# Convolution taps and norm gain loaded as rows and transposed, decay rows laid out by head, and the decay add ordered behind the convolution of k

## The chip, the cores and the metric

The kernel runs on one core of a Trainium2 chip. The metric is device time in microseconds (us) of one execution; lower is better. Three runs of the kernel before gave 1844.48, 1847.61 and 1849.42 us (median 1847.61).

## What is computed

One encoder block on a float32 sequence of 1024 tokens by 1024 channels. Two token mixers read the same normalised input: a gated linear attention (GLA) and a gated DeltaNet (GDN). Their sum is projected and added to the input; a mixture of experts with 32 experts follows, then a last RMSNorm. The change touches the norm's gain and the GDN branch, whose part of the reference is, shortened:

```python
h = rms_norm(x, norm1_w)
proj = h @ w_in
# GDN: centred depthwise convolution of 5 taps on q, k and v, then silu
qkv = silu(centred_depthwise_conv(concat([dq, dk, dv]), conv_w))   # conv_w: [5, 3072]
q, k = l2_norm(q) * dk ** -0.5, l2_norm(k)                         # 8 heads of 128
g = -exp(a_log) * softplus(a + dt_bias)                            # per head and direction
# per chunk, with g the cumulative sum inside the chunk
decay = exp(where(tri, g[..., :, None] - g[..., None, :], 0.0))
lower = strict_lower(k_beta @ k.T * decay)
attn = tri(q @ k.T * decay)
# forward and backward directions, summed
```

## The kernel before, in words

The work is written as straight Python on tiles, and a planner orders it when the program is built: for each engine it makes one fixed list of instructions, by program order and by its own estimate of when operands are ready. On the chip each engine takes its list in order, so an instruction whose operand is late holds everything behind it on that engine. All plain loads and stores are issued by SyncE (SP), also in a fixed order.

Stages: (1) lines 133 to 167 load x in 8 tiles, normalise the rows, turn them with TensorE and split the result into a high and a low part `hT_hi`, `hT_lo`; the norm's gain `n1` is applied per partition at L165 and L166. (2) Lines 205 to 253 make the gates of all GDN heads at once: `gcs` holds the cumulative gates with tokens on partitions and columns in the order direction, chunk, head. TensorE turns it (L249), VectorE copies it out (L251) and SP stores it to device memory as `gcs_d` (L252), one row of 128 floats for each (direction, chunk, head). (3) For each of 8 heads `gdn_stage1` (L282) projects k, convolves it, normalises it, then q, then v, and solves the triangular systems on VectorE; `gdn_stage2` (L400) runs the recurrence over 8 chunks in both directions, and `gdn_stage3` (L498) normalises and stores. Stage 3 of the head before is called inside stage 1 through `finish` (L333). Between the heads `gate_task` (L258) adds projections that only TensorE is long busy with: one behind head 0's stage 1, one behind its stage 2, and two behind each later head while they last. (4) GLA, the output projection, routing, the experts, the last norm.

Each projection (`proj`, L118) is 48 matmuls of 128x128 on 128x512 into two accumulators `pj` (two buffers). Its weights come as two units of 256 KB through `load_w` (L103): load `wraw` (three buffers), cast on ScalarE to `whi` (L112), subtract on VectorE to `wlo` (L114); a later `wraw` load waits for an earlier subtraction.

The convolution (`conv`, L283): ScalarE copies the two accumulators into `cin` (one buffer, L289); VectorE makes one multiply (L292) and four multiply-adds (L294) over 128x1024, each with a tap from `cw[:, wi, j]` as a per-partition scalar; ScalarE takes tanh (L300) and VectorE finishes the silu (L301). TensorE then turns the result for the norm (`sumsq`, L311). `cw` is filled by five loads of one tap each (L188) and `n1` by one (L134); in all six the channel goes to the partition, so consecutive elements in device memory land on different partitions.

The decay (L340 to L346): for each head, half of the chunks (`hf`) and direction (`d`), SP loads four rows of `gcs_d` into `e`, each repeated over all 128 partitions (L342; 128 partitions times 4 runs of 512 bytes, 256 KB); VectorE adds the mask `mneg` (L344); ScalarE takes four exponentials (L346). `e` then scales the Gram matrix of k into `m` (L348), and later the scores of q (L364). `e` has seven buffers, so the loads of the next head's first three tiles are issued as soon as buffers come free.

The lines that set where the add stands:

```python
ka = conv("k", C_DK)
rk, pts = sumsq("k", ka)
...
if finish:
    finish()
...
e = gd.tile([P, 4, P], F32, name="e", bufs=7)
nc.sync.dma_start(e, dap(gcs_d, ...))
ve.tensor_tensor(e, e, mneg[d]..., op=OP.add)
```

Of the kernel before, what the change touches and what calls it, by code (L numbers as in the profile page):

```python
# [8 lines left out]
F32 = mybir.dt.float32  # L9
# [4 lines left out]
OP = mybir.AluOpType  # L14
# [4 lines left out]
P = 128  # L19
D = 1024  # L20
T = 1024
NT = T // P
KD = D // P
# [11 lines left out]
def hybrid_kernel(ctx: ExitStack, tc: tile.TileContext, ins, out):  # L35
# [6 lines left out]
    def dap(t, off, dims):  # L42
        return bass.AP(tensor=t.tensor, offset=t.offset + off, ap=dims)
# [51 lines left out]
    with mix:  # L95
# [34 lines left out]
            return res  # L130


        n1 = cst.tile([P, KD], F32, name="n1")
        nc.sync.dma_start(n1, ins["norm1_w"][0].rearrange("(k p) -> p k", p=P))  # L134
        with tc.tile_pool(name="xp", bufs=1) as xp:
            xt = []
            ssx = xp.tile([P, NT], F32, name="ssx")
            junk = xp.tile([P, D], F32, name="junk", bufs=2)
            for t in range(NT):
                xx = xp.tile([P, D], F32, name=f"xx{t}")  # L140
                nc.sync.dma_start(xx, x[t * P:(t + 1) * P, :])
                xt.append(xx)

            def scale(q):

                for t in (2 * q, 2 * q + 1):
                    sc.activation(junk, xt[t], AF.Square, accum_out=ssx[:, t:t + 1])
                v = small.tile([P, 2], F32, name="vx")
                ve.tensor_scalar(v, ssx[:, 2 * q:2 * q + 2], 1.0 / D, EPS, op0=OP.mult, op1=OP.add)
                rx = rsqrt(v, 2, "x")  # L150
                for i in range(2):
                    t = 2 * q + i
                    ve.tensor_scalar(xt[t], xt[t], rx[:, i:i + 1], None, op0=OP.mult)

            for q in range(4):
                scale(q)
            wfirst = load_w(None, [(0, C_GL, 96), (96, C_AB, 32)])
            for q in range(2):
                for k in range(KD):
                    pt = bank(("tp", "mg")[k % 2], 2)  # L160
                    for i in range(4):
                        te.transpose(pt[:, i, :], xt[4 * q + i][:, k * P:(k + 1) * P], ident)
                    s = slice(q * 512, q * 512 + 512)
                    pf = pt.rearrange("p a b -> p (a b)")
                    sc.activation(hT_hi[:, k, s], pf, AF.Copy, scale=n1[:, k:k + 1])  # L165
                    ve.scalar_tensor_tensor(hT_lo[:, k, s], pf, n1[:, k:k + 1],  # L166
                                            hT_hi[:, k, s].bitcast(F32), op0=OP.mult, op1=OP.subtract)
# [15 lines left out]
        gdn_nw = cst.tile([P, 1], F32, name="gdn_nw")  # L183
        nc.sync.dma_start(gdn_nw, ins["gdn_norm_w"].rearrange("o c -> c o"))
        ve.tensor_scalar(gdn_nw, gdn_nw, 0.25, None, op0=OP.mult)
        cw = cst.tile([P, 24, 5], F32, name="cw")
        for j in range(5):
            nc.sync.dma_start(cw[:, :, j], ins["gdn_conv_w"][0, j].rearrange("(k p) -> p k", p=P))  # L188


        NBs = cst.tile([P, 2, NT, GDN_H], F32, name="NBs")
# [5 lines left out]
        with tc.tile_pool(name="gate", bufs=1) as gpool:  # L197
            glrT = gpool.tile([P, T], F32, name="glrT")
            abT = gpool.tile([P, T], F32, name="abT")
            dt_b = gpool.tile([P, 2, GDN_H], F32, name="dt_b")  # L200
            na = gpool.tile([P, 2, GDN_H], F32, name="na")
            for i, s in enumerate(("fwd", "bwd")):
                nc.sync.dma_start(dt_b[:, i], pbcast(ins[f"gdn_dt_bias_{s}"], GDN_H))
                nc.sync.dma_start(na[:, i], pbcast(ins[f"gdn_a_log_{s}"], GDN_H))
            ps = proj(None, wfirst)
            for hf in range(2):
                s = slice(hf * 512, hf * 512 + 512)
                sc.copy(glrT[0:32, s], ps[hf][0:32])
                ve.tensor_copy(abT[96:128, s], ps[hf][96:128])
            nc.sync.dma_start(glr_d, glrT[0:32])  # L210

            pab = psum.tile([P, NT, 32], F32, name="pab", tag="mg", bufs=2)
            for t in range(NT):
                te.transpose(pab[:, t], abT[96:128, t * P:(t + 1) * P], ident[96:128, 96:128])
            z = gpool.tile([P, 2, 2, NT, GDN_H], F32, name="zg")
            u = gpool.tile([P, 2, 2, NT, GDN_H], F32, name="ug")
            ve.tensor_tensor(z[:, 0].rearrange("p i c h -> p c i h"),
                             pab[:, :, 0:16].rearrange("p c (i h) -> p c i h", i=2),
                             dt_b[:, None, :, :].to_broadcast([P, NT, 2, GDN_H]), op=OP.add)
            ve.tensor_scalar(z[:, 1].rearrange("p i c h -> p c i h"),  # L220
                             pab[:, :, 16:32].rearrange("p c (i h) -> p c i h", i=2), -1.0, None,
                             op0=OP.mult)

            sc.activation(u, z, AF.Abs)
            sc.activation(u, u, AF.Exp, scale=-1.0)
            sc.activation(u, u, AF.Ln, bias=1.0)
            ve.scalar_tensor_tensor(u, z, 0.0, u, op0=OP.max, op1=OP.add)
            sc.activation(na, na, AF.Exp)
            g = gpool.tile([P, 2, NT, GDN_H], F32, name="gg")
            for i in range(2):  # L230
                ve.scalar_tensor_tensor(g[:, i], u[:, 0, i], -1.0,
                                        na[:, i, None, :].to_broadcast([P, NT, GDN_H]),
                                        op0=OP.mult, op1=OP.mult)
            pg = psum.tile([P, 2, 2, NT * GDN_H], F32, name="pg", tag="mg", bufs=2)
            for i in range(2):
                gi = g[:, i].rearrange("p c h -> p (c h)")
                te.matmul(pg[:, 0, i], tri[i], gi, start=True, stop=True)
                te.matmul(pg[:, 1, i], ones, gi, start=True, stop=True)
            fl = lambda t: t.rearrange("p i c h -> p i (c h)")
            ve.tensor_copy(fl(gcs), pg[:, 0])  # L240
            sc.activation(fl(DEC), pg[:, 1], AF.Exp)

            ve.scalar_tensor_tensor(NBs, u[:, 1], -1.0, gcs, op0=OP.mult, op1=OP.subtract)
            ve.tensor_tensor(fl(KT), fl(NBs), pg[:, 1], op=OP.add)
            sc.activation(KT, KT, AF.Exp)
            sc.activation(EG, gcs, AF.Exp)

            prow = bank("mg", 2)
            te.transpose(prow[:, 0], gcs.rearrange("p i c h -> p (i c h)"), ident)  # L249
            grow = gpool.tile([P, P], F32, name="grow")  # L250
            ve.tensor_copy(grow, prow[:, 0])  # L251
            nc.sync.dma_start(gcs_d, grow)  # L252
            ve.tensor_scalar(NEG, EG, -1.0, None, op0=OP.mult)
# [28 lines left out]
        def gdn_stage1(h, finish=None):  # L282
            def conv(nm, c0):  # L283
                ps = proj(c0 + h * P)
                cin = gd.tile([P, T + 4], F32, name="cin", bufs=1)
                gp.memset(cin[:, 0:2], 0.0)
                gp.memset(cin[:, T + 2:T + 4], 0.0)
                for hf in range(2):
                    sc.copy(cin[:, 2 + hf * 512:2 + hf * 512 + 512], ps[hf])  # L289
                wi = {"q": 0, "k": 8, "v": 16}[nm] + h  # L290
                a = gd.tile([P, T], F32, name="acc", bufs=3)
                ve.tensor_scalar(a, cin[:, 0:T], cw[:, wi, 0:1], None, op0=OP.mult)  # L292
                for tp in range(1, 5):
                    ve.scalar_tensor_tensor(a, cin[:, tp:tp + T], cw[:, wi, tp:tp + 1], a,  # L294
                                            op0=OP.mult, op1=OP.add)

                for hf in range(2):
                    s = slice(hf * 512, hf * 512 + 512)
                    th = gt.tile([P, 512], F32, name="gth", bufs=2)
                    sc.activation(th, a[:, s], AF.Tanh, scale=0.5)  # L300
                    ve.scalar_tensor_tensor(a[:, s], th, 1.0, a[:, s], op0=OP.add, op1=OP.mult)  # L301
                return a

            def sumsq(nm, a):
# [12 lines left out]
                return rsqrt(ss, NT, nm), pts  # L317

            ka = conv("k", C_DK)
            rk, pts = sumsq("k", ka)  # L320
            ktok = gd.tile([P, NT, P], F32, name="ktok", bufs=2)
            kch = gd.tile([P, NT, P], F32, name="kch", bufs=2)
# [13 lines left out]
            for hf in range(2):  # L336
# [2 lines left out]
                    te.matmul(pgm[:, i], kch[:, 4 * hf + i], kch[:, 4 * hf + i], start=True, stop=True)  # L339
                for d in range(2):  # L340
                    e = gd.tile([P, 4, P], F32, name="e", bufs=7)
                    nc.sync.dma_start(e, dap(gcs_d, ((d * NT + 4 * hf) * GDN_H + h) * P,  # L342
                                             [[0, P], [GDN_H * P, 4], [1, P]]))
                    ve.tensor_tensor(e, e, mneg[d][:, None, :].to_broadcast([P, 4, P]), op=OP.add)  # L344
                    for i in range(4):
                        sc.activation(e[:, i], e[:, i], AF.Exp, bias=NBs[:, d, 4 * hf + i, h:h + 1])  # L346
                    m = gd.tile([P, 4, P], F32, name="m", bufs=6)
# [867 lines left out]
```

## Time and profile before

| | |
|---|---|
| median of the three runs | 1847.61 us |
| the profiled execution's own time | 1845.9 us |
| its span from first to last instruction | 1844.1 us |
| TensorE matmul busy | 1684.2 us (91% of the span) |
| VectorE busy | 1326.0 us (72%) |
| ScalarE busy | 918.2 us (50%) |
| mean granted TensorE clock | 0.974 of full speed |

The span is 1.8 us shorter than the execution's own time. Engines in the rows are PE (TensorE matmul), PEld (TensorE weight load), DVE (VectorE), ACT (ScalarE), POOL (GpSimd) and SPq (SyncE's list of loads and stores). In a timeline row the columns are the start and the duration in us, the engine, the line, the operation, output and inputs, and how many were merged; in brackets stands how long the engine was idle just before, and what ended that. Where `x` and `ns` stand, they are a count and a mean. Matmuls overlap, so the durations of single ones add up to more than the time in which they ran.

### The profile page before, as it was taken

To read this page: it belongs to the slowest core of one execution; us is meant where nothing else is said; L and a number is where in the kernel's file an instruction comes from. 1 tells how busy PE (TensorE), PEld (TensorE's weight loads), DVE (VectorE), ACT (ScalarE), POOL (GpSimd) and SP (SyncE) were. 2 spreads that over 40 slices of the span, in tenths; PEclk is the share of its full clock that TensorE was granted. 3 is DMA by queue.
4 is the path that set the end of the run, shared out by engine and by line. 5 is a ranking of instruction groups with operands and counts; after the bars stand their busy time and mean duration, and the time that the engine had idled before them with its cause. 6 is when DMAs were issued, how large, how long until landed. Compare 5 with 4: busy or idle time off the path is not lost. (4 is left out here: it accounts for less than half of the span.)

```text
span 1844.1 us, 27107 instructions
## 1 busy us (share of the span) xinstructions
PE 1684.2 (91%) x9582; PEld 1378.5 (75%) x9582; DVE 1326.0 (72%) x2998; ACT 918.2 (50%) x1913; POOL 177.6 (10%) x184
## 2 busy tenths in 40 slices
PE   6799899899999999999999999998999799888880
PEld 4587777787888888888888778887778587666660
DVE  6589695787687787877855355655778797777773
ACT  5434435254362453534434344534435687777762
POOL 0000000000000000000000000000000143334430
PEclk9899999999999999999999999999999899999996
DMA  6322223322323222231222112312677699999965
GB/s 148 64 71 61 65 55 79 69 57 77 74 58 97 52 75 69 69 93 45 66 69 74 43 44 75 95 55 78 208 230 252 215 345 312 311 321 326 330 202 199
DMA packets 236298, 241.02 MB, mean 131 GB/s; under 512 B 89136, under 2 KB 187712, under 8 KB 236160
## 3 DMA queue, kind: packets, MB, share of 16 engines
q1 hardware_dynamic: 226944, 222.46, 39.0%
q0 software_dynamic: 9216, 16.81, 4.0%
q8 instruction: 76, 1.25, 0.3%
q14 instruction: 62, 0.51, 0.1%
HBM read 205.44 MB, written 50.53 MB: 139 GB/s over the span
## 5 line engine op out<-in xcount | busy, mean ns | idle before, releaser
L80 PE MATMUL pj<-hT_hi,whi 128*128 128x512 f32 x1168 | 472.2, 404 | 2.8 <-ACT cin L289 2.4
L81 PE MATMUL pj<-hT_lo,whi 128*128 128x512 f32 x1168 | 472.3, 404 | 0.0
L82 PE MATMUL pj<-hT_hi,wlo 128*128 128x512 f32 x1168 | 471.6, 404 | 0.5 <-DVE wlo L114 0.5
L1044 DVE TENSOR_TENSOR elo<-eraw,ehi 128x2048 fp32r<-128x2048 f32 x96 | 219.5, 2288 | 70.9 <-ACT ehi L1043 68.2
L80 PEld LDWEIGHTS pj<-hT_hi,whi 128*128 128x128 f32 x1168 | 222.1, 190 | 43.9 <-ACT cin L289 3.2
L82 PEld LDWEIGHTS pj<-hT_hi,wlo 128*128 128x128 f32 x1168 | 222.0, 190 | 39.4 <-DVE wlo L114 1.2
L81 PEld LDWEIGHTS pj<-hT_lo,whi 128*128 128x128 f32 x1168 | 222.3, 190 | 37.5
L1043 ACT CAST ehi<-eraw 128x2048 fp32r<-128x2048 f32 x96 | 184.5, 1922 | 69.9 <-DMA eraw<-in_moe_w_up_dram 65.1
L112 ACT CAST whi<-wraw 128x512 fp32r<-128x512 f32 x146 | 90.6, 620 | 190.3 <-PE pj L81 177.0
L114 DVE TENSOR_TENSOR wlo<-wraw,whi 128x512 fp32r<-128x512 f32 x146 | 100.0, 686 | 93.0 <-ACT whi L112 83.8
L294 DVE SCALAR_TENSOR_TENSOR acc<-cin,cw,acc 128x1024 f32<-128x1024 f32 x96 | 122.5, 1276 | 0.7
L80 PE MATMUL pgu<-ehi,xh 128*128 128x512 f32 x256 | 105.3, 411 | 0.0
L1095 POOL DMA_INDIRECT acc_d<-y,idx x32 | 84.1, 2627 | 199.2 <-DMA acc_d<-y,idx 72.3
L81 PE MATMUL pgu<-elo,xh 128*128 128x512 f32 x256 | 102.1, 399 | 0.0
L82 PE MATMUL pgu<-ehi,xl 128*128 128x512 f32 x256 | 101.9, 398 | 0.0
L391 DVE TENSOR_TENSOR prod<-V,X 128x2 f32<-128x2 f32 (+30 forms) x248 | 85.5, 345 | 5.9
L393 DVE TENSOR_REDUCE V<-prod 128x1 f32<-128x2 f32 (+30 forms) x248 | 84.4, 340 | 6.1
L266 ACT ACTIVATE gth<-pj 128x512 f32<-128x512 f32 x64 | 38.1, 595 | 75.9 <-PE pj L82 75.4
L1050 POOL DMA_INDIRECT xb<-h_d,idx x32 | 59.2, 1850 | 149.6 <-ACT xb L1105 132.6
L346 ACT ACTIVATE e<-e,NBs 128x128 f32<-128x128 f32 x128 | 44.0, 396 | 34.0 <-DVE e L344 34.0
L473 ACT ACTIVATE kt<-ktok,KT 128x128 f32<-128x128 f32 x112 | 44.7, 402 | 30.8 <-PE cb L474 13.5
L82 PEld LDWEIGHTS pgu<-ehi,xl 128*128 128x128 f32 x256 | 48.7, 190 | 11.8
(405 smaller groups left out, 3268.2 us busy)
## 6 DMA issues: line engine op xcount, KB each, us to landing
wraw<-in_w_in_dram SPq DMA_DIRECT2D x144, 256.0 KB, 3.0
eraw<-in_moe_w_gate_dram SPq DMA_DIRECT2D x64, 512.0 KB, 15.9
eraw<-in_moe_w_up_dram SPq DMA_DIRECT2D x64, 512.0 KB, 17.7
eraw<-in_moe_w_down_dram SPq DMA_DIRECT2D x32, 1024.0 KB, 19.1
e<-gcs_d SPq DMA_DIRECT2D x32, 256.0 KB, 6.0
gate_d<-gateT SPq DMA_DIRECT2D x16, 512.0 KB, 3.6
xx<-in_x_dram SPq DMA_DIRECT2D x8, 512.0 KB, 7.7
gin<-gate_d SPq DMA_DIRECT2D x8, 512.0 KB, 3.2
```

Of the source, the lines that this page charges most:

```text
L80: te.matmul(o, lh, rh, start=start, stop=False)
L81: te.matmul(o, lh, rl, start=False, stop=False)
L82: te.matmul(o, ll, rh, start=False, stop=stop)
L112: sc.copy(hi, raw)
L114: ve.tensor_tensor(lo, raw, hi.bitcast(F32), op=OP.subtract)
L294: ve.scalar_tensor_tensor(a, cin[:, tp:tp + T], cw[:, wi, tp:tp + 1], a, op0=OP.mult, op1=OP.add)
L391: ve.tensor_tensor(pr_[:, :mc, :i + 1], V[:, :mc, :i + 1], X[:, i, :i + 1][:, None, :].to_broadcast([P, mc, i + 1]), op=OP.mult)
L393: ve.tensor_reduce(V[:, :mc, i], pr_[:, :mc, :i + 1], axis=AX.X, op=OP.add)
L1043: sc.copy(hi, raw)
L1044: ve.tensor_tensor(lo, raw, hi.bitcast(F32), op=OP.subtract)
L1050: gp.indirect_dma_start(out=xb, out_offset=None, in_=h2_d[:, :], in_offset=bass.IndirectOffsetOnAxis(ap=si, axis=0), bounds_check=T - 1, o ...
L1095: gp.indirect_dma_start(out=acc_d[:, :], out_offset=bass.IndirectOffsetOnAxis(ap=si, axis=0), in_=y, in_offset=None, bounds_check=T - 1, o ...
```

## The change

- `n1` and the taps `cw` become columns of one tile `cols` (128x128). Two loads bring 8 rows of the norm's gain and 120 rows of the taps (5 taps times 24 blocks of 128 channels), 512 bytes a row, into `rows`; TensorE turns the tile and ScalarE copies it out. These instructions stand ahead of the loads of x. The six loads of before are gone.
- Ahead of the turn of the cumulative gates VectorE copies them into the order head, direction, chunk. A row of `gcs_d` is now (head, direction, chunk), so the four rows of one `e` lie next to each other, and a load of `e` is 128 runs of 2 KB.
- The add on `e` gets an ordering edge: on VectorE it stands behind the last instruction of this head's convolution of k.

```diff
-        n1 = cst.tile([P, KD], F32, name="n1")
-        nc.sync.dma_start(n1, ins["norm1_w"][0].rearrange("(k p) -> p k", p=P))
+        cols = cst.tile([P, P], F32, name="cols")
+        n1 = cols[:, 0:KD]
         with tc.tile_pool(name="xp", bufs=1) as xp:
+            rows = xp.tile([P, P], F32, name="rows")
+            nc.sync.dma_start(rows[0:KD], ins["norm1_w"][0].rearrange("(k p) -> k p", p=P))
+            nc.sync.dma_start(rows[KD:P], ins["gdn_conv_w"][0].rearrange("j (k p) -> (j k) p", p=P))
+            pt = bank("tp", 2)
+            te.transpose(pt[:, 0], rows, ident)
+            sc.copy(cols, pt[:, 0])
...
-        cw = cst.tile([P, 24, 5], F32, name="cw")
-        for j in range(5):
-            nc.sync.dma_start(cw[:, :, j], ins["gdn_conv_w"][0, j].rearrange("(k p) -> p k", p=P))
+        def cw(i, j):
+            return cols[:, KD + 24 * j + i:KD + 24 * j + i + 1]
...
-            te.transpose(prow[:, 0], gcs.rearrange("p i c h -> p (i c h)"), ident)
+            ghead = gpool.tile([P, GDN_H, 2, NT], F32, name="ghead")
+            ve.tensor_copy(ghead.rearrange("p h i c -> p i c h"), gcs)
+            te.transpose(prow[:, 0], ghead.rearrange("p h i c -> p (h i c)"), ident)
...
-                ve.tensor_scalar(a, cin[:, 0:T], cw[:, wi, 0:1], None, op0=OP.mult)
+                ve.tensor_scalar(a, cin[:, 0:T], cw(wi, 0), None, op0=OP.mult)
...
-                    ve.scalar_tensor_tensor(a[:, s], th, 1.0, a[:, s], op0=OP.add, op1=OP.mult)
+                    conv.last = ve.scalar_tensor_tensor(a[:, s], th, 1.0, a[:, s], op0=OP.add, op1=OP.mult)
...
             ka = conv("k", C_DK)
+            k_done = conv.last.ins
...
-                    nc.sync.dma_start(e, dap(gcs_d, ((d * NT + 4 * hf) * GDN_H + h) * P,
-                                             [[0, P], [GDN_H * P, 4], [1, P]]))
-                    ve.tensor_tensor(e, e, mneg[d][:, None, :].to_broadcast([P, 4, P]), op=OP.add)
+                    nc.sync.dma_start(e.rearrange("p a b -> p (a b)"),
+                                      dap(gcs_d, ((2 * h + d) * NT + 4 * hf) * P, [[0, P], [1, 4 * P]]))
+                    with tc.issue_after(k_done):
+                        ve.tensor_tensor(e, e, mneg[d][:, None, :].to_broadcast([P, 4, P]), op=OP.add)
```

## Rows read from the trace of the kernel before

**Rows 1.** Stretches: start:end, length; busy us: PE, PEld, DVE, ACT, POOL; PEclk, DMA, GB/s.

```profile
300.00:400.00 100.00, 92.19 (x581) 76.06 (x581) 77.17 (x193) 40.62 (x118) 2.66 (x11) 0.98 0.32 73
...
700.00:800.00 100.00, 99.80 (x655) 83.33 (x654) 76.83 (x201) 47.93 (x144) 3.36 (x13) 1.00 0.28 72
```

**Rows 2.** Timeline, PE: the instructions that followed its gaps up to 451 us.

```profile
31.39 0.44 PE L162 MATMUL mg<-ident,xx 128*128 128x128 f32 x2 [2.35 <-DVE hT_lo L166]
...
78.51 0.87 PE L311 MATMUL tp<-ident,acc 128*128 128x128 f32 x3 [11.31 <-issue]
...
228.42 0.90 PE L513 MATMUL mg<-ident,oac 128*128 128x128 f32 x3 [4.08 <-DVE oac L511]
...
343.37 0.94 PE L513 MATMUL mg<-ident,oac 128*128 128x128 f32 x4 [5.12 <-DVE oac L511]
...
450.54 0.66 PE L513 MATMUL mg<-ident,oac 128*128 128x128 f32 x4 [2.02 <-DVE oac L511]
```

**Rows 3.** Timeline, ACT and DVE, 56 to 79 us: head 0's convolution of k.

```profile
56.65 0.58 ACT L289 COPY cin<-pj 128x512 f32<-128x512 f32 x1
...
58.66 0.69 DVE L344 TENSOR_TENSOR e<-e,mneg 128x512 f32<-128x512 f32 x1 [3.91 <-DMA e<-gcs_d]
...
62.40 0.69 DVE L344 TENSOR_TENSOR e<-e,mneg 128x512 f32<-128x512 f32 x1 [3.04 <-DMA e<-gcs_d]
63.01 0.74 DVE L292 TENSOR_SCALAR acc<-cin,cw 128x1024 f32<-128x1024 f32 x1
...
67.55 0.69 DVE L344 TENSOR_TENSOR e<-e,mneg 128x512 f32<-128x512 f32 x1 [0.36 <-DMA e<-gcs_d]
...
77.72 1.28 DVE L301 SCALAR_TENSOR_TENSOR acc<-gth,acc 128x512 f32<-128x512 f32 x2
```

**Rows 4.** Groups by line: busy us, mean ns, then idle before and its releaser.

```profile
L294 DVE SCALAR_TENSOR_TENSOR acc<-cin,cw,acc 128x1024 f32<-128x1024 f32 x96 | 122.5, 1276 | 0.7
...
L344 DVE TENSOR_TENSOR e<-e,mneg 128x512 f32<-128x512 f32 x32 | 22.0, 689 | 31.3 <-DMA e<-gcs_d 31.3
```

**Rows 5.** Timeline, DVE: the adds on e ahead of the gap at 224 us.

```profile
220.42 0.69 DVE L344 TENSOR_TENSOR e<-e,mneg 128x512 f32<-128x512 f32 x1 [2.11 <-DMA e<-gcs_d]
...
223.43 0.69 DVE L344 TENSOR_TENSOR e<-e,mneg 128x512 f32<-128x512 f32 x1 [1.96 <-DMA e<-gcs_d]
```

**Rows 6.** Stretches after three of the gaps (columns as in rows 1).

```profile
78.50:84.20 5.70, 5.69 (x18) 4.74 (x19) 5.56 (x7) 4.57 (x24) 0.00 (x0) 0.51 0.18 46
228.40:234.40 6.00, 5.98 (x18) 5.07 (x19) 4.91 (x12) 0.59 (x1) 0.00 (x0) 0.51 0.40 134
343.40:347.00 3.60, 3.60 (x13) 3.18 (x14) 2.54 (x6) 0.09 (x1) 0.00 (x0) 0.53 0.08 28
```

**Rows 7.** Timeline, 14 to 30 us, and the packets of 12 to 32 us.

```profile
DMA packets 19445, 1.94 MB, mean 97 GB/s; under 512 B 17771, under 2 KB 19307, under 8 KB 19444
...
23.99 3.57 SPq L109 DMA_DIRECT2D wraw<-in_w_in_dram  x3
...
29.35 0.62 ACT L112 CAST whi<-wraw 128x512 fp32r<-128x512 f32 x1 [3.55 <-DMA wraw<-in_w_in_dram]
```

**Rows 8.** DMA issues: count, KB each, median us to landing.

```profile
wraw<-in_w_in_dram SPq DMA_DIRECT2D x144, 256.0 KB, 3.0
...
e<-gcs_d SPq DMA_DIRECT2D x32, 256.0 KB, 6.0
...
n2r<-in_norm_w_dram SPq DMA_DIRECT2D x1, 512.0 KB, 5.7
```

**Rows 9.** A stretch of head 1's convolutions, and the PE gap in it.

```profile
125.00:150.00 25.00, 22.93 (x106) 18.69 (x105) 24.38 (x44) 7.34 (x20) 0.13 (x2) 1.00 0.25 68
...
146.42 0.50 PE L80 MATMUL pj<-hT_hi,whi 128*128 128x512 f32 x1 [2.06 <-ACT cin L289]
```

**Rows 10.** Timeline: a 128x128 copy on DVE, and ACT's first square.

```profile
49.76 0.29 DVE L240 COPY gcs<-pg 128x128 f32<-128x128 f32 x1 [1.06 <-PE pg L238]
...
5.06 1.06 ACT L147 ACTIVATE junk<-xx 128x1024 f32<-128x1024 f32 x1 [3.04 <-DMA xx<-in_x_dram]
```

More of the change, by code (lines that the diff above doesn't have):

```diff
@@ L291, in conv @@
                 a = gd.tile([P, T], F32, name="acc", bufs=3)
-                ve.tensor_scalar(a, cin[:, 0:T], cw[:, wi, 0:1], None, op0=OP.mult)
+                ve.tensor_scalar(a, cin[:, 0:T], cw(wi, 0), None, op0=OP.mult)
                 for tp in range(1, 5):
-                    ve.scalar_tensor_tensor(a, cin[:, tp:tp + T], cw[:, wi, tp:tp + 1], a,
+                    ve.scalar_tensor_tensor(a, cin[:, tp:tp + T], cw(wi, tp), a,
                                             op0=OP.mult, op1=OP.add)
```

## The prediction

> **What bounds the kernel now.** I first cut the span into stretches. TensorE is the bound from 500 to 1000 us: in 700 to 800 us it is busy for 99.8 of 100 us, and nothing the change does there can shorten it. Between 300 and 400 us it is busy for only 92.19 [rows 1]. So whatever there is to win lies before 500 us, and I next read TensorE's timeline there for gaps. Four of its large gaps, and one at the start, end on something that the change touches: 2.35 us at 29 us, 11.31 at 67 us, 4.08 at 224, 5.12 at 338 and 2.02 at 448 us [rows 2].
>
> The largest is named "issue", so I followed its operand `acc`, head 0's convolved k. Its inputs were complete at 57.23 us (56.65 plus 0.58). But in VectorE's list the adds on `e` stand ahead of and between the steps of the convolution, and they waited for their loads: 3.91 and 3.04 us before the first step started at 63.01, and more between the later ones; the last step came at 77.72 [rows 3]. Over the whole kernel the 32 adds cost 22.0 us of work and 31.3 us of VectorE standing still for these loads [rows 4]. The gaps at 224, 338 and 448 us wait for VectorE's L511 (stage 3 of the head before). Ahead of the first of them two adds waited 2.11 and 1.96 us, together 4.07 against a gap of 4.08 [rows 5, 2]; the same pattern of late adds stands before the other two.
>
> The gaps also cost clock. After three of them TensorE's granted clock is 0.51 to 0.53 of full speed, the lower level of 1.2 GHz, for 5.7, 6.0 and 3.6 us of nearly full work [rows 6], where a stretch without such a gap has 1.00, the level of 2.4 GHz [rows 1].
>
> The gap at 29 us has another source. From 12 to 32 us the queue moves 19,445 packets, 17,771 of them under 512 bytes [rows 7]; by the code 5 x 3072 are single taps of 4 bytes. The next weights were issued only at 23.99 us, and ScalarE stood 3.55 us until they landed at 29.35, with the split of `hT_hi` behind them in its list [rows 7].
>
> **The change part by part.**
>
> Taps and gain as rows. It removes the six loads of 4-byte elements (16,384 of them) and adds two loads of 128 rows, one turn on TensorE and one 128x128 copy on ScalarE. SP is moved past nothing but x: x is issued behind two loads instead of one, yet no longer behind 1024 single elements, and I cost that at nothing between those two. The copy is about as long as VectorE's of this size, 0.29 us, and fits in the 3.04 us that ScalarE idles before its first square [rows 10]; if the rows landed later than x, every square would start late by that. With the taps gone the weights can go as soon as a buffer is free, and ScalarE's wait should go. TensorE then gains its 2.35 us; between 0 and ScalarE's 3.55. I take -2.4.
>
> Head 0. Without adds ahead of it, the convolution takes one step of 0.74 and four of 1.276 [rows 3, 4], 5.84 us, to 63.1; two tanh and the two halves of the last step (1.28) end near 65.5. TensorE has work until about 67.2 (78.51 less 11.31), so the whole gap is covered. What is late next is the next projection's accumulator, which waits for `cin`; where that happens now in head 1, TensorE stood 2.06 us [rows 9]. So -11.3 + 2.1 = -9.2 (0 to -11.3). The 5.7 us at half clock become 2.85: -2.8 (0 to -2.85).
>
> Heads 1 to 3. The adds that waited belonged to a later head and did not have to be done yet; behind that head's convolution of k they are long landed. The gaps of 4.08, 5.12 and 2.02 us go: -11.2 (0 to -11.2). Half clock after them, (6.0 + 3.6) / 2 = -4.8 (0 to -4.8). From head 4 on TensorE is full, so nothing is won.
>
> What the moved adds cost. Three adds per head leave the recurrence, where VectorE has room, for the convolutions, where in head 1 it is busy 24.38 of 25 us [rows 9]. That is 3 x 0.689 = 2.07 us a head [rows 4]. In heads 4 to 7 TensorE's full list covers it. In heads 1 to 3 it could stand in full (6.2), or not at all; I take half, +3.1. If the cover is gone everywhere it is 7 x 2.07 = 14.5. The four exponentials of each tile follow the adds; the Gram matrix that they are needed with comes only after sum of squares, inverse root and two turns, so I cost them at nothing.
>
> Gates by head. One more strided copy on VectorE, 0.29 us by the nearest copy [rows 10], delays the store of `gcs_d` and the first `cin` copy behind it: +0.3 (0 to 1). The loads of `e` become 128 runs of 2 KB for 512 of 512 bytes. Today they take 6.0 us to landing, where weights of the same 256 KB in 512-byte runs take 3.0, so neither bytes nor packet size alone explains it; the one broadcast with long runs, 512 KB, took 5.7 [rows 8]. Between 3 and 6 us I take 3, which costs nothing more, as the adds are no longer early.
>
> By a rule of the Trainium skill ("DMA: Bandwidth & Descriptors", Anatomy of one DMA and Specifications) a load costs about 2.0 us plus its bytes over 436 GB/s, and runs of 512 bytes are already at line rate; by it longer runs would change nothing. The 6.0 against 3.0 us speak against the first half of it for this load; no row here shows the second.
>
> Sum: -2.4 - 9.2 - 2.8 - 11.2 - 4.8 + 3.1 + 0.3 = -27.0. From the profiled execution's 1845.9 that gives 1818.9; the median of the runs shown stands 1.7 above it, so I expect 1820.6, say **1820.5**. With the best ends (-3.55 - 11.3 - 2.85 - 11.2 - 4.8) it is -33.7, 1814. The planner remakes every list, and waits of one or two us come and go with that; the forecast's own range is 1808 to 1831.
>
> **The rivals.**
>
> Longer runs do not help: the loads of `e` still take 6.0 us. Then the fourth of head 0's adds, which could start at 67.55 [rows 3], is some 2.4 us behind k's end, and q's convolution behind it. For it: the same row is still read 128 times. Against: the adds are no longer in front of anything that TensorE waits for at once. 1820.5 + 2.4 = 1823. Chance 0.13. By the page's rule above the loads would not change either.
>
> The gaps of heads 1 to 3 come back as waits for `cin` in the convolutions, since VectorE is full there: 11.2 + 4.8 are lost again. For it: 24.38 of 25 us and the 2.06 us wait [rows 9]. Against: in heads 4 to 7 the same work leaves TensorE at 99.8 [rows 1]. 1836.5. Chance 0.13.
>
> The change does not do what it says: the planner puts other late work where the adds stood, or head 0 waits for the next weights instead, and only the start is won: 1847.6 - 2.4 = 1845. Against: nothing else in those lists waits for so long. Chance 0.07.
>
> Slower: in each of the eight heads four adds now stand right behind k's convolution, ahead of the inverse root that k's normalisation needs, and TensorE runs dry for 4 x 0.689 = 2.8 us and then loses 2.8 more at half clock, as after the gap of head 0 [rows 6]. 8 x 5.6 = 44.8 against 30.4 of gains (all of the terms with a minus): +14.4 and the 0.3, 1862. It decides once a head loses over 30.4 / 8 = 3.8 us. Against: the squares on ScalarE come first, and VectorE fills their time with the adds. Chance 0.09.
>
> **How the numbers follow.** Forecast 0.58, the rivals 0.13, 0.13, 0.07 and 0.09. A measurement of this kernel can tell about 0.3%, 5.5 us, from no change. Faster by more than that (under 1842): the forecast and the first two rivals, less a tail, 0.83. Within it: the third and that tail, 0.08. Slower: 0.09. The range from 1808 to 1845 leaves out the slower case, half of the third and the ends of the forecast, just under 0.2.
>
> **What would show it.** In the profile after: no load of taps between 14 and 24 us, no wait of ScalarE on `wraw` at 29; all steps of head 0's convolution together on VectorE, the turn of k at 63 to 65 us without a gap before it; the adds' wait for `e` down from 31.3 us to under 5; no gap of over 2 us before L513; TensorE's clock at full speed from about 30 to 500 us. I am wrong if TensorE's share between 100 and 500 us does not rise, if a gap of like size stands at another line in head 0, or if waits for `cin` grow past 6 us.

## The result and the profile after

| | before | after |
|---|---|---|
| median of 4 runs each, us | 1846.30 | 1817.35 |
| lowest to highest, us | 1844.48 to 1849.42 | 1814.81 to 1819.27 |
| ratio, 95% interval | | 0.9841 [0.9821, 0.9860] |
| the profiled execution's own time and span, us | 1845.9, 1844.1 | 1817.02, 1815.2 |

Faster by 1.6%, 3 us below the forecast of 1820.5. TensorE's busy time over the whole span is unchanged (1684.2 us before, 1684.3 after), so what went is idle time:

The first row of the page after (busy us, share of the span, instructions).

```profile
PE 1684.3 (93%) x9583; PEld 1382.0 (76%) x9583; DVE 1329.9 (73%) x2999; ACT 911.6 (50%) x1914; POOL 166.4 (9%) x184
```

I cut each span at the first cumulative-gate matmul (`pg`) and at the first `pz` matmul of the second mixer, the GLA, behind the last GDN head. First the kernel before (columns as in [rows 1]), then after:

```profile
48.62:1019.35 970.73, 934.58 (x5759) 769.31 (x5759) 735.33 (x1840) 422.57 (x1217) 33.45 (x111) 0.99 0.27 68
1019.35:1844.10 824.75, 718.96 (x3684) 586.24 (x3684) 560.61 (x1060) 467.50 (x650) 143.70 (x68) 0.96 0.61 204
```

```profile
46.28:992.02 945.74, 931.44 (x5769) 768.39 (x5769) 739.58 (x1842) 416.09 (x1219) 34.23 (x111) 0.99 0.26 70
992.02:1815.20 823.18, 722.03 (x3674) 590.17 (x3674) 559.91 (x1059) 467.25 (x648) 131.77 (x68) 0.95 0.62 204
```

Of the 28.9 us of span, 2.3 were won ahead of `pg` (48.62 to 46.28), 25.0 in the eight GDN heads (970.73 to 945.74) and 1.6 behind them. In the heads TensorE's idle time fell from 36.15 us (970.73 less 934.58) to 14.30 (945.74 less 931.44); the other 3.1 of the 25.0 are busy time (934.58 to 931.44). Behind the heads the busy time rose by as much (718.96 to 722.03).

Next the timeline of VectorE in head 0, after, in the place of [rows 3].

```profile
55.22 0.75 DVE L301 TENSOR_SCALAR acc<-cin,cols 128x1024 f32<-128x1024 f32 x1
56.01 5.32 DVE L303 SCALAR_TENSOR_TENSOR acc<-cin,cols,acc 128x1024 f32<-128x1024 f32 x4
62.02 1.29 DVE L310 SCALAR_TENSOR_TENSOR acc<-gth,acc 128x512 f32<-128x512 f32 x2 [0.70 <-ACT gth L309]
63.23 2.49 DVE L355 TENSOR_TENSOR e<-e,mneg 128x512 f32<-128x512 f32 x4
65.64 0.68 DVE L114 TENSOR_TENSOR wlo<-wraw,whi 128x512 fp32r<-128x512 f32 x1
68.68 0.17 DVE L325 TENSOR_SCALAR ssk<-ssk 128x8 f32<-128x8 f32 x1 [2.36 <-ACT jk L323]
...
72.31 0.74 DVE L301 TENSOR_SCALAR acc<-cin,cols 128x1024 f32<-128x1024 f32 x1
```

The steps of k's convolution stand together and the adds follow at 63.23 without a wait. But VectorE then idles 2.36 us for the squares, and q's convolution starts only at 72.31, behind k's whole inverse root. The group of the adds (against [rows 4]) and the loads of `e` (against [rows 8]):

```profile
L355 DVE TENSOR_TENSOR e<-e,mneg 128x512 f32<-128x512 f32 x32 | 21.1, 684 | 1.6 <-DMA e<-gcs_d 1.5
```

```profile
e<-gcs_d SPq DMA_DIRECT2D x32, 256.0 KB, 3.1
```

VectorE's wait fell from 31.3 to 1.6 us, the landing from 6.0 to 3.1. Last, the four TensorE gaps over 1.5 us that are left between 46 and 1000 us (timeline), and stretches behind the first three and one full one:

```profile
83.09 0.63 PE L320 MATMUL tp<-ident,acc 128*128 128x128 f32 x4 [2.79 <-DVE acc L310]
...
134.85 0.50 PE L80 MATMUL pj<-hT_hi,whi 128*128 128x512 f32 x1 [2.76 <-ACT cin L298]
...
244.04 0.50 PE L80 MATMUL pj<-hT_hi,whi 128*128 128x512 f32 x1 [2.04 <-ACT cin L298]
...
992.02 0.95 PE L616 MATMUL pz<-ws,gs 98*128 98x256 f32 x4 [3.93 <-DVE ws L605]
```

```profile
83.09:88.80 5.71, 5.71 (x29) 5.11 (x30) 4.58 (x8) 3.55 (x18) 0.00 (x0) 0.70 0.59 148
134.85:140.00 5.15, 5.15 (x20) 4.34 (x21) 4.97 (x9) 5.01 (x25) 1.01 (x5) 0.67 0.49 82
244.00:249.00 5.00, 4.96 (x15) 3.93 (x16) 5.00 (x9) 0.47 (x1) 0.22 (x2) 0.66 0.30 78
300.00:400.00 100.00, 99.64 (x652) 82.83 (x651) 82.28 (x216) 43.96 (x144) 4.39 (x12) 1.00 0.29 77
```

The gaps of 11.31, 4.08, 5.12 and 2.02 us [rows 2] are gone, and 300 to 400 us is full. New are a wait for q's accumulator in head 0 and longer waits for `cin`, and the stretch of 5 to 6 us behind each of the three has a mean granted clock of 0.66 to 0.70, part of it at the lower level of 1.2 GHz.

### The profile page after: what moved, and what is told of

It reads as the page before. It is cut to its first block, busy times and chain, and to the rows that moved or that the text cites. A ratio compares the mean times of both kernels' runs of the same rounds, so it can differ in the third digit from the quotient of the medians.

```text
span 1815.2 us, 27128 instructions
## 1 busy us (share of the span) xinstructions
PE 1684.3 (93%) x9583; PEld 1382.0 (76%) x9583; DVE 1329.9 (73%) x2999; ACT 911.6 (50%) x1914; POOL 166.4 (9%) x184
## 5 line engine op out<-in xcount | busy, mean ns | idle before, releaser
L303 DVE SCALAR_TENSOR_TENSOR acc<-cin,cols,acc 128x1024 f32<-128x1024 f32 x96 | 122.6, 1277 | 0.9
L1106 POOL DMA_INDIRECT acc_d<-y,idx x32 | 71.3, 2227 | 213.0 <-ACT hh L1093 60.4
L484 ACT ACTIVATE kt<-ktok,KT 128x128 f32<-128x128 f32 x112 | 44.1, 401 | 28.9 <-PE cf L485 14.0
L80 PEld LDWEIGHTS pgu<-ehi,xh 128*128 128x128 f32 x256 | 50.2, 196 | 10.9 <-ACT xh L1073 0.2
```

The lines of the kernel that those rows point to most:

```text
L80: te.matmul(o, lh, rh, start=start, stop=False)
L303: ve.scalar_tensor_tensor(a, cin[:, tp:tp + T], cw(wi, tp), a, op0=OP.mult, op1=OP.add)
L1106: gp.indirect_dma_start(out=acc_d[:, :], out_offset=bass.IndirectOffsetOnAxis(ap=si, axis=0), in_=y, in_offset=None, bounds_check=T - 1, o ...
```

## The experiments

The change has three parts: **taps** (rows turned by TensorE), **layout** (gates by head, one piece of 2 KB per load) and **edge** (adds behind the convolution of k). Twelve kernels ran in three sets of four; the median of before was 1846.96, 1847.23 and 1844.31 us in the sets, so I compare by ratios, not by medians, across sets. "Wait" is VectorE's idle time ahead of the adds, "landing" the median time of the loads of `e` from issue to landing (32 loads; the profile shows the landing of 14 to 16 of them), "GLA" the start of the first `pz` matmul of the second mixer in the profiled run. Behind that matmul the code is the same in every kernel, yet the rest of the span in the profiled runs goes from 818.7 us (e10) to 827.4 (e2). So a few us in the heads are better read from the start of the GLA than from a time.

| kernel | median us | ratio, 95% interval | wait | landing | GLA |
|---|---|---|---|---|---|
| before | | | 31.3 | 6.0 | 1019.35 |
| e1: taps | 1841.60 | 0.9971 [0.9959, 0.9982] | 31.7 | 6.0 | 1014.86 |
| e2: layout | 1810.38 | 0.9805 [0.9787, 0.9822] | 4.8 | 3.3 | 985.30 |
| e3: edge | 1823.28 | 0.9868 [0.9847, 0.9889] | 10.2 | 5.4 | 998.02 |
| e4: taps, edge | 1823.72 | 0.9872 [0.9852, 0.9892] | 9.9 | 5.3 | 998.06 |
| e5: layout, edge | 1816.28 | 0.9835 [0.9809, 0.9860] | 1.9 | 3.3 | 992.94 |
| e6: taps, layout | 1810.65 | 0.9800 [0.9779, 0.9821] | 4.7 | 3.3 | 984.44 |
| after (all three) | 1817.35 | 0.9841 [0.9821, 0.9860] | 1.6 | 3.1 | 992.02 |
| a2: after again | 1813.30 | 0.9829 [0.9816, 0.9843] | 1.7 | 3.2 | 990.99 |
| e7: e6 with 512-byte pieces | 1815.32 | 0.9829 [0.9807, 0.9851] | 11.1 | 4.0 | 990.18 |
| e8: e6, two `cin` | 1813.99 | 0.9826 [0.9805, 0.9847] | 8.3 | 3.3 | 988.41 |
| e9: after, edge in head 0 only | 1807.04 | 0.9808 [0.9785, 0.9831] | 2.8 | 3.3 | 984.16 |
| e10: after, edge in heads 1 to 7 only | 1810.19 | 0.9816 [0.9803, 0.9830] | 4.0 | 3.2 | 987.11 |
| e12: e1 with 64 bytes behind each row | 1813.77 | 0.9831 [0.9818, 0.9844] | 7.6 | 3.7 | 987.92 |

### e1, taps alone

```diff
-        n1 = cst.tile([P, KD], F32, name="n1")
-        nc.sync.dma_start(n1, ins["norm1_w"][0].rearrange("(k p) -> p k", p=P))
...
+            nc.sync.dma_start(rows[0:KD], ...)
+            nc.sync.dma_start(rows[KD:P], ...)
+            te.transpose(pt[:, 0], rows, ident)
+            sc.copy(cols, pt[:, 0])
...
-        for j in range(5):
-            nc.sync.dma_start(cw[:, :, j], ...)
```

> The kernel before with the first part alone: taps and gain loaded as rows and turned. Gates stored as before, adds left where the planner puts them. Order theory (the place of the adds in VectorE's list gives nearly everything): only the start moves, about -2.4 us, 1844, ratio 0.9987; the gap of some 11 us in head 0 and the three of 2 to 5 us behind it stay. Rival, small loads (the 16,384 single-element reads hold up more than the next weights, and part of head 0's late e loads is their doing): -5 us or more, and the wait of VectorE for e falls well below 31.3 us.

Measured: 5.4 us faster (3.3 to 7.6 by the interval), so more than the -2.4 of the start; but the wait for `e` did not move (31.7), and head 0's gap stands at 11.17 us. The rival fails in its second half: the small loads don't slow the loads of `e`. The extra came at the start itself, where `pg` moved from 48.62 to 44.59. It does not last: beside the layout the taps bring `pg` 2.2 us forward (47.60 in e2, 45.37 in e6), the GLA 0.9, and the median nothing (e6 against e2). One place where it goes can be seen. Both kernels have the same gap for `cin` in head 1, and the stretch behind it is at full clock (2.4 GHz) in e2 and has a mean clock of 0.66 in e6. First the timeline row and the stretch of e2, then of e6:

```profile
132.20 0.50 PE L80 MATMUL pj<-hT_hi,whi 128*128 128x512 f32 x1 [2.05 <-ACT cin L291]
```

```profile
132.20:137.20 5.00, 5.00 (x26) 4.16 (x27) 4.43 (x9) 3.92 (x18) 0.00 (x0) 1.00 0.49 103
```

```profile
130.09 0.52 PE L80 MATMUL pj<-hT_hi,whi 128*128 128x512 f32 x1 [2.05 <-ACT cin L297]
```

```profile
130.10:135.10 5.00, 5.00 (x19) 4.03 (x20) 4.29 (x7) 2.95 (x13) 0.00 (x0) 0.66 0.49 104
```

In these 5.00 us TensorE ran 26 matmuls in e2 and 19 in e6; at 0.34 below full speed e6 loses 1.7 us there. One execution of each was profiled, so whether this belongs to the kernel or to that execution is not shown.

### e2, layout alone

```diff
-            te.transpose(prow[:, 0], gcs.rearrange("p i c h -> p (i c h)"), ident)
+            ve.tensor_copy(ghead.rearrange("p h i c -> p i c h"), gcs)
+            te.transpose(prow[:, 0], ghead.rearrange("p h i c -> p (h i c)"), ident)
...
-                    nc.sync.dma_start(e, dap(gcs_d, ((d * NT + 4 * hf) * GDN_H + h) * P,
-                                             [[0, P], [GDN_H * P, 4], [1, P]]))
+                    nc.sync.dma_start(e.rearrange("p a b -> p (a b)"),
+                                      dap(gcs_d, ((2 * h + d) * NT + 4 * hf) * P, [[0, P], [1, 4 * P]]))
```

> The kernel before with the second part alone: cumulative gates stored by head, so that each e is 2 KB in one piece; adds where the planner puts them, taps as before. Loads of e should land after about 3 us in place of 6. Order theory: the adds still stand ahead of head 0's convolution and still wait for their loads, 3 us less for each that stands first; VectorE's wait for e falls from 31.3 us to about 12 to 18, the gap of head 0 from 11.3 to 5 to 8 us, and the time by 8 to 14 us, 1832 to 1838. Rival, speed theory (late loads were the whole cause, and landing at 3 us is enough by itself): VectorE's wait below 5 us and the time within 5 us of the changed kernel plus 2.4, 1820 to 1825.

Measured: 1810.38, better than either theory and by the ratio below the whole change (0.9805 against 0.9841, intervals that touch). The order theory falls: without any edge, the wait is 4.8 us. The timeline of VectorE in head 0 of e2 shows why:

```profile
55.27 0.69 DVE L346 TENSOR_TENSOR e<-e,mneg 128x512 f32<-128x512 f32 x1 [1.35 <-DMA e<-gcs_d]
55.94 0.69 DVE L114 TENSOR_TENSOR wlo<-wraw,whi 128x512 fp32r<-128x512 f32 x1
56.55 0.74 DVE L294 TENSOR_SCALAR acc<-cin,cw 128x1024 f32<-128x1024 f32 x1
57.22 0.68 DVE L346 TENSOR_TENSOR e<-e,mneg 128x512 f32<-128x512 f32 x1
...
66.21 1.28 DVE L303 SCALAR_TENSOR_TENSOR acc<-gth,acc 128x512 f32<-128x512 f32 x2
67.42 0.74 DVE L294 TENSOR_SCALAR acc<-cin,cw 128x1024 f32<-128x1024 f32 x1
```

The adds stand ahead of and between the steps just as in [rows 3], but from the second on they find their data and cost only their own 0.68 us. k's last step starts 4.2 us later than after's (62.02), 1.3 of them from a later `pg` (47.60 against 46.28), and still in time for TensorE: the gap before k's turn is 0.64 us. And q's convolution starts at 67.42, 4.9 us earlier than after.

### e3, edge alone, and e4, edge and taps

```diff
             ka = conv("k", C_DK)
+            k_done = conv.last.ins
...
-                    ve.tensor_tensor(e, e, mneg[d][:, None, :].to_broadcast([P, 4, P]), op=OP.add)
+                    with tc.issue_after(k_done):
+                        ve.tensor_tensor(e, e, mneg[d][:, None, :].to_broadcast([P, 4, P]), op=OP.add)
```

> The kernel before with the third part alone: the decay adds issued behind the convolution of k; loads of e stay in four pieces of 512 bytes at about 6 us, taps as before. Order theory: -22 to -26 us, 1820 to 1824; no gap over 3 us in head 0, VectorE's wait for e below 8 us. Speed theory: the adds of heads 0 to 3 still wait, now behind the convolution, and hold up the next one; less than 12 us is won, 1834 or more.

> The changed kernel without its second part: taps and gain as rows, adds behind the convolution of k, but gates stored as before, so that e lands after about 6 us. Order theory: within 3 us of the changed kernel (1817 to 1821), since no add is early any more. Speed theory: over 12 us behind it, 1829 or more. If the first two parts' gains add up, this stands 2.4 us below the third part alone.

Measured: the edge alone gives 23.7 us (ratio 0.9868) and takes the gap of 11.3 us away while the loads still need 5.4 us; so it works, as the order theory said, though the wait (10.2) missed its bound of 8. With the taps added it is the same (0.9872); at 1823.72 e4 lies between its two expectations (up to 1821, from 1829), and its GLA starts 6.0 us behind that of after, so the slow loads still cost something behind the edge. Edge and layout are two cures of one wait: alone 24 and 37 us, together 31 (e5 below), and with the taps 29 (after) and 31 (a2).

### e5 and e6, the other two pairs

Their diffs are those above, put together.

> The changed kernel without its first part: gates by head and the edge, taps and gain as single elements. Edge theory: the gaps of the changed kernel at head 0's q (about 2.8 us), at head 1's and 2's cin (2.8 and 2.0) and before the second mixer (3.9) are all here, and the time is the changed kernel's plus 0 to 5 us, 1817 to 1822. Rival, planner's chance: other gaps at other lines, and a time anywhere from 1808 to 1822. If the taps are worth nothing beside the edge, as the fourth run suggests (1823.7 against 1823.3), it stands at 1817.

> The changed kernel without its third part: adds where the planner puts them. Edge theory (with loads at 3 us the edge behind the convolution of k no longer saves anything, and it costs: it leaves VectorE idle for some 5 us before that convolution's end and pushes four adds and the convolution of q behind it, which brings the gaps of 2.79, 2.76 and 3.93 us): this kernel gives the second part's -36 and the first part's -5 together, 1805 to 1808, about 10 us faster than the changed kernel. Rival, chance of the planner's list (the second part alone happened to get a good list; parts do not add): within 3 us of the changed kernel, 1814 to 1821, with gaps over 2.5 us of its own.

Measured: e5 has the changed kernel's gaps, 2.80, 2.79, 2.08 and 3.93 us, and its time. In e6 two of over 1.5 us are left, 2.04 for `cin` and this one:

```profile
984.44 0.70 PE L613 MATMUL pz<-ws,gs 98*128 98x256 f32 x4 [1.91 <-DVE ws L602]
```

With the layout in place, kernels with the edge stand at 0.9835, 0.9841 and 0.9829, those without at 0.9805 and 0.9800; the GLA starts at 991 to 993 us against 984 to 985. The intervals touch, yet the five traces agree: next to the layout the edge costs some 0.3 to 0.4%, 5 to 7 us. That the taps would add to the layout missed (1805 to 1808 expected, 1810.65 measured), and so did the rival (1814 to 1821).

### e9 and e10, the edge by heads, beside a2

```diff
-                    with tc.issue_after(k_done):
+                    with tc.issue_after(k_done) if h == 0 else ExitStack():
```

(e10 has `h > 0`; a2 is the changed kernel as it is.)

> The changed kernel itself, beside the three that follow: 1814 to 1819, with the gaps of 2.8 (q of head 0), 2.8 and 2.0 (cin of heads 1 and 2) and 3.9 us (before the second mixer) again.

> The changed kernel with the edge in head 0 alone; adds of heads 1 to 7 where the planner puts them. Edge theory: what the edge costs lies where VectorE has no slack. The gap of 2.8 us at head 0's q and half clock behind it stay (4.5 us in all), the others go back to what they are without the edge: about 1814.5, half way between. Rival, planner's chance: gaps at other lines than these.

> The changed kernel with the edge in heads 1 to 7 alone; head 0's adds where the planner puts them. Edge theory: no gap at head 0's q; gaps at cin of heads 1 and 2 (2.8 and 2.0) and before the second mixer (3.9, of which 1.9 is there without the edge) stay, with half clock behind them: 1814 to 1816. If head 0 alone had been the cost, 1810.5.

Measured, by the GLA's start: no edge 984.44, head 0 only 984.16, heads 1 to 7 only 987.11, both 990.99. All three medians lie below what was expected (1813.30, 1807.04 and 1810.19), so my sum of single gaps was wrong. e9 has the worst gap of all in head 0:

```profile
84.02 1.23 PE L320 MATMUL tp<-ident,acc 128*128 128x128 f32 x8 [3.88 <-DVE acc L310]
```

and starts head 1 4.7 us behind e6 (its convolution of k at 125.48 against 120.75), yet head 4 at 451.40 against 451.23. So heads 1 to 3 make good what head 0 loses when their adds are left to the planner; that this is because VectorE is free there is my reading. With the edge in them too, a2 stays 3.7 to 4.1 us behind e10 from head 1 to the end. In heads 1 to 7 the edge by itself costs 2.7 us, 2.0 of them in the gap before `pz` (3.93 against 1.91). In times the three are apart by less than their intervals (0.9829, 0.9808, 0.9816).

### e7 and e12, what makes the loads slow

e7 is e6 and e12 is e1, each with a DRAM tensor in which every row of 512 bytes is followed by 64 unused bytes. e12:

```diff
-    gcs_d = dram.tile([P, P], F32, name="gcs_d")
+    gcs_d = dram.tile([P, P + 16], F32, name="gcs_d")
...
-                    nc.sync.dma_start(e, dap(gcs_d, ((d * NT + 4 * hf) * GDN_H + h) * P,
-                                             [[0, P], [GDN_H * P, 4], [1, P]]))
+                    nc.sync.dma_start(e, dap(gcs_d, ((d * NT + 4 * hf) * GDN_H + h) * (P + 16),
+                                             [[0, P], [GDN_H * (P + 16), 4], [1, P]]))
```

> The first two parts without the edge, as in e6_taps_layout, but each row of gates in DRAM is followed by 64 unused bytes, so that an e is again loaded in four pieces of 512 bytes, which lie side by side. It tells the length of the pieces from their place. If length decides, the loads land after 5 to 6 us and VectorE's wait for e comes back to 20 us or more, 1825 or slower. If place decides (rows of one head near each other rather than 4 KB apart), they land after 3 to 3.5 us and the time is that of e6_taps_layout within 3 us.

> The kernel before with the first part (taps as rows) and the gates still stored by chunk, but each row of gates in DRAM followed by 64 unused bytes, so that the four pieces of an e lie 4608 bytes apart and not 4096. Distance theory (pieces far apart are slow): landing stays at 6 us, head 0's seven loads at some 85 GB/s, time 1839 to 1843 as with the taps alone. Stride theory (the exact step of 4096 bytes is what is slow): landing 4 us and 250 to 340 GB/s, as with pieces side by side, and 1814 to 1820 without any other change.

Measured: in e12 the pieces are as short as before and as far apart, 4608 bytes for 4096, and 1.4%, some 26 us, go against e1 (0.9971 to 0.9831), as the stride theory said. Head 0 shows it, in the view of DMA from 48 to 75 us, 40 slices of 0.675 us: what the engines moved, and the median landing of the seven loads of `e` (the profile shows four of the seven in each). First before, then e12:

```profile
GB/s 0 0 0 0 0 77 20 0 46 90 86 84 86 20 62 81 60 70 38 83 72 83 88 173 270 251 152 131 166 127 97 83 61 71 54 94 90 115 125 114
...
e<-gcs_d SPq DMA_DIRECT2D x7, 256.0 KB, 13.9
```

```profile
GB/s 0 38 59 0 30 173 153 231 183 338 329 223 314 309 319 297 222 14 0 5 155 227 1 0 0 84 295 9 0 0 0 0 43 266 80 0 0 0 0 0
...
e<-gcs_d SPq DMA_DIRECT2D x7, 256.0 KB, 5.5
```

Before, the engines never move more than 90 GB/s between 53 and 63 us (slices 9 to 22), and the loads pile up to 13.9 us; with 64 bytes more per row it is 223 to 338 GB/s in slices 10 to 16, and 5.5 us. A load of `e` with no other one beside it shows the step too, but less: 4.5 us before (issued at 414 us), 3.2 in e12 (387 us). Piece length counts for little: pieces of 512 bytes land after 4.0 us (e7, 576 bytes apart) or 3.7 (e12, 4608 apart), one piece of 2 KB after 3.3 (e6), the old layout after 6.0. So e7's two expectations both missed, half way: its landing is 4.0, its wait 11.1. That last 0.4 to 0.7 us is worth some 5 us to a kernel without the edge (e7 0.9829 against e6 0.9800, intervals overlapping).

### e8, a try for a faster kernel

```diff
-                cin = gd.tile([P, T + 4], F32, name="cin", bufs=1)
+                cin = gd.tile([P, T + 4], F32, name="cin", bufs=2)
...
-                    e = gd.tile([P, 4, P], F32, name="e", bufs=7)
+                    e = gd.tile([P, 4, P], F32, name="e", bufs=6)
...
-                    m = gd.tile([P, 4, P], F32, name="m", bufs=6)
+                    m = gd.tile([P, 4, P], F32, name="m", bufs=5)
```

(From e6; the tile `xb` that shares `cin`'s buffer has two as well.)

> The first two parts without the edge, and cin in two buffers; to make room, e has 6 buffers for 7 and m 5 for 6. A try for a faster kernel. If the wait for cin (2.05 us at 130 us and half clock behind it in the second part's run) is still worth its gap, -2 to -5 us against e6_taps_layout, near 1802. If the buffers taken from e matter more (the next head's adds then start one later), +2 or more, with waits of VectorE for e over 5 us.

Measured: the `cin` gap is gone, the wait for `e` is 8.3 for 4.7 us, and the time is 3.3 us above e6 (intervals overlap; the GLA starts 4.0 later): the second case. The expectation took the clock behind the gap from e2 as half; in e2 it is 1.00, as shown above, so there was less to win than it said. The fastest versions that ran are e6 and e2 (0.9800 and 0.9805) and e9 (0.9808), which can't be told apart.

## Why the prediction was right, and where it was not

**The number** (1820.5, measured 1817.35) and the side were right, and most of the signs named in it are there: no wait of ScalarE on `wraw`, the convolution in one piece, the adds' wait 1.6 us, no gap over 2 us ahead of the turns in stage 3 (0.7 us in all, 11.7 before), waits for `cin` under 6 us (4.8). Full clock to 500 us is not there, and where I had counted on one new gap, of 2.1 us, there are two (2.79 and 2.04) and two that grew (to 2.76 and 3.93). That the total came within 3 us is in part luck: below, one part is 5.0 us dearer than costed, and 6.8 us went that the sum did not hold.

**The start** (-2.4): `pg` came 2.3 us earlier. As a share of the end time it is not safe: alone the taps gave 5.4 us, beside the other parts nothing that was measured.

**Head 0** (-9.2): 11.31 went and 2.79 came. I had named `cin` as late next, with 2.1 us; it was q's own convolution, held behind the adds and k's inverse root. The slower case had named a gap of 2.8 us in every head, from four adds ahead of the inverse root; this one of 2.79 is not it, since the adds end at 65.72 (63.23 plus 2.49) and VectorE is idle for 2.36 us before the inverse root starts at 68.68. Half clock after it (-2.8): the stretch behind the new gap is at 0.70, so about -1.1.

**Heads 1 to 3** (-11.2 and -4.8): both as said, and 300 to 400 us is now as full as the heads behind it.

**The moved adds** (+3.1) were sized too small. The step said that they would stand in full convolutions. They did: the `cin` gaps grew from 2.06 to 2.76 plus 2.04 us (+2.7), two stretches of 5 us at 0.66 to 0.67 behind them cost 1.7 us each (a third of the clock lost; +3.4), and the gap before `pz` grew from 1.98 to 3.93 (+2.0): +8.1. The waits for `cin` and the clock behind them are the second rival's mechanism, at 6.1 of its 16.0 us. This was hidden in the total because small gaps, which I had not counted, went as well: without the named ones (26.57 us before, 11.52 after) the idle time of the heads is 9.58 and 2.78 us, so 6.8 went there. With these sizes the terms to the GLA's start are -2.3 - 8.5 - 1.1 - 11.2 - 4.8 + 8.1 = -19.8, with the small gaps -26.6, of the measured -27.3.

**The step that failed is the cause.** I wrote that the adds' place in VectorE's list was what cost, credited -28.0 to the edge, and costed the layout at +0.3; landing at 3 us, I wrote, "costs nothing more, as the adds are no longer early". As a statement about the edge alone it holds (e3, -24). But the adds stood badly only because their loads were slow (in head 0 at 90 GB/s or less). With that mended by the layout (e2, e6) the wait is under 5 us in the planner's own order, that order is the better one, and the edge costs 5 to 7 us. With it mended by 64 bytes (e12) the kernel without layout and edge is as fast as the changed one (0.9831 against 0.9841 and 0.9829); the edge beside the 64 bytes was not tried. The first rival, loads still at 6 us behind the edge, was priced well: 1823, and e4, the changed kernel without the layout, took 1823.72 with loads of 5.3 us.

I had seen 6.0 us against 3.0 for equal bytes in equal pieces [rows 8], and asked only whether length or the repeated row was the reason. What differed too was the step between the pieces: GDN_H x 512 = 4096 bytes. The weights share part of this: by the code the four pieces of one partition lie 128 rows of `w_in` (9280 floats, 37,120 bytes) apart, which is 1160 times 4096 bytes, and they land in 3.0 us. But there every partition reads rows of its own; in a load of `e` all 128 partitions read the same four pieces. So a step that is a multiple of 4096 bytes is not slow in every load.

Of the rule of the Trainium skill that the prediction drew on ("DMA: Bandwidth & Descriptors"), the half on length (Specifications), by which runs of 512 bytes are already at line rate, is nearly borne out once the step is not 4096 bytes: such pieces landed after 3.7 and 4.0 us, one of 2 KB after 3.3. The half on the 2.0 us (Anatomy of one DMA) was measured on loads issued by GpSimd, while those here are issued by SyncE. Nearer to this case is a row on the same page of the Trainium skill (Latency and other measured facts): tiles in HBM whose rows, one per partition, lie a large power of two apart are slow to copy, from a pitch of 512 KiB up; 4 KiB more per row brought the full rate back at 4 MiB, 192 bytes did not, and the reason that it gives is called unverified. Here the step is 4096 bytes, it lies between the pieces that one partition reads, and 512 bytes more suffice, so whether it is the same effect is not shown. Why 4096 bytes is slow was not tried, nor other steps, nor that step with 128 different rows in place of one row read 128 times.

## What to carry to other kernels

When a load takes longer than another of the same size, look at the step between its pieces, and at how many partitions read the same ones, before reordering its readers: next to the taps 64 bytes of padding were worth more (e12, 0.9831) than an order written by hand (e4, 0.9872). Try each part of a change alone; two cures of one wait do not add, and the second may leave only its price. And a gap need not cost its length in the end: in e9 head 1 starts 4.7 us late and head 4 only 0.2.

## What was not expected of the hardware

The step of 4096 bytes, in loads whose 128 partitions all read the same pieces: 6.0 us per load and 13.9 for the first seven, issued within 11 us, against 3.7 and 5.5 at 4608 bytes. The clock: a gap of 2.05 us was followed by a clock of 1.00 in e2 and 0.66 in e6, at the same line, and one before q's turn in head 0 by 1.00 in e3 (2.78 us) and 0.66 in e4 (2.79 us), over the 5 us behind it. So the price of a gap of that length is not fixed: nothing, or 1.7 us more.
